# Output projection by Strassen's seven products, as a stage of its own behind the input projection, with low weight parts kept in DRAM

## The chip, the cores and the metric

The kernel runs on one core of a Trainium2 chip. The metric is the device time of one execution in microseconds; lower is better. TensorE (PE) multiplies, VectorE (DVE), ScalarE (ACT) and GpSimd (POOL) do the elementwise work, and SyncE (SP) issues the DMAs, which move data between DRAM and on-chip SBUF.

## The reference

One decoder layer in float32 on x, 2048 rows by 2048 channels. Cut to what matters:

```python
proj = einsum("bsd,de->bse", x, w_in) + b_in          # 2048 x 2048 times 2048 x 5376
c_val, c_glu, c_gate, q, k, v, a_gate = split(proj)
y_conv = conv_branch(c_val, c_glu) * silu(c_gate)     # depthwise conv of width 31, LayerNorm, silu
y_attn = windowed_attention(q, k, v, sinks) * silu(a_gate)
y = concatenate([y_conv, y_attn])                     # 2048 x 2048
y = einsum("bse,ed->bsd", y, w_out) + b_out           # 2048 x 2048 times 2048 x 2048
return layer_norm(2 ** 0.25 * x + y, ln_g, ln_b)
```

## The kernel before

The rows are worked off in four chunks of 512 (`SC`). A chunk has 84 steps of input projection and 32 steps of output projection, and then the next chunk follows. Every step takes one weight tile of 128 x 1024 float32 and has 24 matmuls of 128 x 128 by 128 x 512.

**High and low parts.** Each float32 operand is split into a high part (`copy` on ACT, rounded to fp32r) and a low part (`lo_part`: the value minus the high part, L117). A product is three matmuls (`mm3`, L527 to L529): high by high, high by low, low by high. Weights come in whole (`load_w`, 3 buffers `wr`), and `split_w` makes `wh` on ACT (L114) and `wl` on POOL for the input projection and on DVE for the rest, 3 buffers each. Every weight of the input projection is so loaded and split once a chunk, four times in all.

**Input projection.** Eight `first` steps make four column tiles side by side in four PSUM banks; 76 `in` steps then make one column tile in two steps each. `evac_in` takes a finished tile out of PSUM. Attention blocks are put between steps by the table `att`; convolution and norm work stands in a background queue `bg`, from which `run_bg` takes a few pieces a step.

**Output projection.** The products y (`ys`, high and low parts, 16 tiles each) stay in SBUF. For each of four column blocks of 512, eight steps accumulate 4 row tiles of 128 over all 16 tiles of y (`out_mm`). `evac_out` adds PSUM to the prepared 2^0.25 x + b_out (L409) and takes its statistics (L412). After a chunk, `out_norm` puts 16 norm units (ACT, DVE L436, POOL L437, store L441) into `bg`, so they run in the next chunk's first steps. In the very last column block the row tiles are finished one after the other, each with its own `tail_norm`.

**Buffers and queues.** 69 slots of 128 x 512 float32 hold everything that isn't a weight. All DMAs are issued by SP, in one order; each engine's instructions are issued in one order too. The main loop runs at each step n:

```python
list(load_w(n + 3))
split_w(n + 2)
```

## Time and profile before

| | |
|---|---|
| median of 3 runs | 2747.06 us (2746.41 to 2747.39) |
| the profiled execution: its time / its span | 2745.35 us / 2743.6 us |
| PE busy | 2696.2 us, 98% of the span |
| DVE, ACT, POOL busy | 71%, 41%, 41% |
| DMA | 308.53 MB, 112 GB/s over the span |
| weight tiles loaded, 512 KB each | 464: 336 for `w_in` (84 a chunk), 128 for `w_out` |

Busy shares are averages over the span. An engine that is idle costs nothing unless another waits for it; so the table says which engine is loaded, and the waits say what the time hangs on.

### The profile page before, as it was taken

The page shows a single profiled execution, that of the slowest core. Times are in us where ns is not written, and L with a number is a line of the kernel's source. Part 1 is how long each engine was busy: PE and PEld are TensorE (multiplying, and loading weights), DVE is VectorE, ACT ScalarE, POOL GpSimd, SP SyncE. Part 2 cuts the span into 40 slices and gives each one's busy share as a digit, 9 for nine tenths or more (in the row PEclk, how much of TensorE's full clock was granted, in tenths as well). Part 3 has the DMA queues.
Part 4 walks back from the last instruction along what each step waited for, and adds up shares of the span by engine and source line. Part 5 has one row for each costly group of instructions (what it writes and reads, how often), then busy time and mean ns, then how long its engine had stood idle before and what let it go on. Part 6 is the DMA issues. An engine that isn't in the chain of part 4 may idle for free.

```text
span 2743.6 us, 33348 instructions
## 1 busy us (share of the span) xinstructions
PE 2696.2 (98%) x12448; PEld 2243.1 (82%) x12448; DVE 1952.4 (71%) x2986; ACT 1120.5 (41%) x2060; POOL 1118.7 (41%) x632
## 2 busy tenths in 40 slices
PE   9999999999999999999999999999999999999996
PEld 7888888888788888878878888887887888888885
DVE  5587877754857887775585779777457677986827
ACT  4344454522434445442243443544233345444422
POOL 2455555200645555610064555560006455556002
PEclk9999999999999999999999999999999999999998
DMA  5222222364422222235442222224544222222424
GB/s 179 96 89 85 79 91 92 100 208 145 148 91 92 85 78 93 85 129 189 142 153 87 90 77 85 92 86 147 171 150 146 85 92 85 77 92 86 158 99 142
DMA packets 101826, 308.53 MB, mean 112 GB/s; under 512 B 11296, under 2 KB 11424, under 8 KB 101664
## 3 DMA queue, kind: packets, MB, share of 16 engines
q1 hardware_dynamic: 101664, 306.40, 33.2%
q8 instruction: 98, 1.61, 0.2%
q14 instruction: 64, 0.52, 0.1%
HBM read 289.58 MB, written 16.78 MB: 112 GB/s over the span
## 4 chain that ended last, share of the span: by engine, by line
PE 90%; DVE 4%; issue 2%; ACT 2%; POOL 1%; DMA 1%; SPq 0%; DVEq 0%; POOLq 0%
PE in L529 21%; PE in L527 21%; PE in L528 21%; PE out L527 7%; PE out L529 7%; PE out L528 7%; PE pv L334 2%; PE sc L284 1%; PE sc L285 1%; PE pt L311 1%; POOL vsum L248 1%; DMA xn<-in_x_dram 1%; DVE wl L117 1%; DVE xn L436 0%; DVE xn L565 0%
## 5 line engine op out<-in xcount | busy, mean ns | idle before, releaser
L529 PE MATMUL in<-xh,wl 128*128 128x512 f32 x2688 | 1050.3, 391 | 10.9 <-DVE wl L117 10.9
L527 PE MATMUL in<-xh,wh 128*128 128x512 f32 x2688 | 1053.8, 392 | 5.6 <-ACT xh L114 5.6
L528 PE MATMUL in<-xl,wh 128*128 128x512 f32 x2688 | 1049.5, 390 | 0.0
L117 POOL TENSOR_TENSOR wl<-wr,wh 128x1024 fp32r<-128x1024 f32 x304 | 746.7, 2459 | 637.6 <-ACT wh L114 602.9
L114 ACT ACTIVATE wh<-wr 128x1024 fp32r<-128x1024 f32 (+1 forms) x467 | 488.6, 1050 | 824.8 <-PE out L529 345.8
L203 DVE SCALAR_TENSOR_TENSOR cv<-h,cst,cv 128x512 f32<-128x512 f32 x896 | 632.1, 746 | 2.3
L529 PEld LDWEIGHTS in<-xh,wl 128*128 128x128 f32 x2688 | 505.8, 188 | 119.1 <-DVE wl L117 12.6
L527 PEld LDWEIGHTS in<-xh,wh 128*128 128x128 f32 x2688 | 506.5, 188 | 106.2 <-ACT xh L114 5.6
L528 PEld LDWEIGHTS in<-xl,wh 128*128 128x128 f32 x2688 | 506.1, 188 | 101.6 <-DVE xl L117 0.5
L117 DVE TENSOR_TENSOR wl<-wr,wh 128x1024 fp32r<-128x1024 f32 (+1 forms) x163 | 214.1, 1316 | 255.3 <-ACT wh L114 250.7
L437 POOL TENSOR_TENSOR xn<-xn,b 128x512 f32<-128x512 f32 x48 | 85.8, 1819 | 582.9 <-DVE xn L436 582.9
L527 PE MATMUL out<-wh,yah 128*128 128x512 f32 x512 | 199.7, 391 | 4.0 <-DVE xn L409 4.0
L528 PE MATMUL out<-wl,yah 128*128 128x512 f32 x512 | 199.3, 389 | 0.0
L527 PE MATMUL out<-wh,ych 128*128 128x512 f32 x512 | 199.2, 389 | 0.0
L528 PE MATMUL out<-wl,ych 128*128 128x512 f32 x512 | 199.2, 389 | 0.0
L529 PE MATMUL out<-wh,ycl 128*128 128x512 f32 x512 | 199.2, 389 | 0.0
L529 PE MATMUL out<-wh,yal 128*128 128x512 f32 x512 | 198.6, 389 | 0.0
L299 ACT ACTIVATE pr<-pr,sm 128x128 f32<-128x128 f32 x256 | 99.8, 391 | 165.9 <-DVE sm L295 165.9
L527 PEld LDWEIGHTS out<-wh,yah 128*128 128x128 f32 x512 | 96.1, 188 | 27.1 <-DVE xn L409 6.3
L529 PEld LDWEIGHTS out<-wh,yal 128*128 128x128 f32 x512 | 96.1, 188 | 20.1
L529 PEld LDWEIGHTS out<-wh,ycl 128*128 128x128 f32 x512 | 96.1, 188 | 20.0
L527 PEld LDWEIGHTS out<-wh,ych 128*128 128x128 f32 x512 | 96.1, 188 | 20.0
...
## 6 DMA issues: line engine op xcount, KB each, us to landing
wr<-in_w_in_dram SPq DMA_DIRECT2D x304, 512.0 KB, 3.2
wr<-in_w_out_dram SPq DMA_DIRECT2D x128, 512.0 KB, 3.3
...
wr<-in_w_first_dram SPq DMA_DIRECT2D x31, 512.0 KB, 3.7
...
```

The lines of the kernel that those rows point to most:

```text
L114: A.activation(out=dst, in_=src, func=AF.Copy)
L117: eng.tensor_tensor(out=dst, in0=src, in1=hi.bitcast(F32), op=ALU.subtract)
L203: V.scalar_tensor_tensor(out=o, in0=h[:, t:t + SC], scalar=wt(t), in1=a, op0=ALU.mult, op1=ALU.add)
L248: G.tensor_tensor(out=s, in0=st["vsum"], in1=q, op=ALU.add)
L284: T.matmul(o, qs[:, b * P:(b + 1) * P], ks[kv][:, b * P:b * P + 256], start=True, stop=False)
L285: T.matmul(o, qs[:, b * P:(b + 1) * P], kl[kv][:, b * P:b * P + 256], start=False, stop=True)
L299: A.activation(out=p3[:, u, :], in_=p3[:, u, :], func=AF.Exp, scale=HD ** -0.5, bias=sm[:, 1, u:u + 1], accum_out=sm[:, 3, u:u + 1])
L334: T.matmul(o, l, m, start=(n == 0), stop=(n == len(mm) - 1))
L437: G.tensor_tensor(out=z, in0=z, in1=st["b", d], op=ALU.add)
L527: T.matmul(o, lh, mh, start=start, stop=False)
L528: T.matmul(o, lh, ml, start=False, stop=False)
L529: T.matmul(o, ll, mh, start=False, stop=stop)
```

## The change

The step order becomes four chunks of 84 input steps, and behind them 112 output steps. The output stage has two blocks of 1024 rows. In a block, y and `w_out` are cut into halves by rows, by the inner dimension and by columns; seven products of half size (in the order 1, 2, 6, 7, 4, 5, 3) take the place of eight. Each product has 8 steps (two column blocks `dp` of 512, four steps `p` each), of 24 matmuls.

- y goes to DRAM (`store_y`), and `gen_y` loads what a product needs, adds or subtracts it, and splits the sum, for the product after the one that runs.
- The sums of weight quarters are made in the chunks 1 to 3 (`tsum_part`, POOL and ACT) and kept in DRAM with the low parts of all seven operands (`tsum`, `olo`).
- The low parts of the input weights are made in chunk 0 only and stored (`wlo`); later chunks load them (`load_lo`), as does the output stage.
- `evac_out` adds a product to the one or two results that take it; 8 finished tiles of a block wait in DRAM (`zd`) for their norm. Two groups of four banks take turns.
- The last four column tiles of a chunk are made side by side in 8 `last` steps, each step's weight in four DMAs, so that tiles of x come free one by one.
- Stores are issued two steps after their data is made (`store_later`).

The norms of the chunks 1, 0 and 3 begin with the third product of block 0, the first of block 1 and the third product (last in order) of block 1; that of chunk 2 is the tail.

The diff, cut to its core:

```diff
@@ -30,6 +30,8 @@
 KT = D // P
 NSLOT = 69
+PRODS = (1, 2, 6, 7, 4, 5, 3)
...
-    def four_banks(name):
+    def left_banks(name):
         return [f(f"{name}_{i}") for i, f in enumerate((acc_bank, acc_bank, cv_bank, cv_bank))]
+    def score_banks(name):
+        sc = ps_sc.tile([P, 2, 512], F32, tag="sc", name=f"{name}_s")
+        return [sc[:, 0, :], sc[:, 1, :]]
+    def right_banks(name):
+        return score_banks(name) + [ps_pt.tile([P, 512], F32, tag="pt", name=f"{name}_t"),
+                                    ps_pv.tile([P, 512], F32, tag="pv", name=f"{name}_v")]
...
             return f
-        bg_late = []
-        bg.extend(fin(j) for j in range(8))
+        st["fins"] = [fin(j) for j in range(8)]
...
-                ys[c, e] = (slot(f"yah{c}_{e}", F32R), slot(f"yal{c}_{e}", F32R))
-            hi, lo = ys[c, e]
-            V.tensor_tensor(out=o[:, i, :], in0=o[:, i, :], in1=st["ag", e][:, cols], op=ALU.mult)
-            copy(hi[:, cols], o[:, i, :])
-            lo_part(V, lo[:, cols], o[:, i, :], hi[:, cols])
+                yr[c, e] = slot(f"ya{c}_{e}")
+            V.tensor_tensor(out=yr[c, e][:, cols], in0=o[:, i, :], in1=st["ag", e][:, cols], op=ALU.mult)
+            if b == NB - 1:
+                store_y(c, e, yr.pop((c, e)))
...
-    def evac_out(c, d, s, ps):
-        z = st["z", c, s, d] = st["xn", s]
-        V.tensor_tensor(out=z, in0=z, in1=ps, op=ALU.add)
...
+    def load_xn(c, s, d):
+        t = st["zx", c, s, d] = slot(f"xn{c}_{s}_{d}")
+        r = c * SC + s * P
+        nc.sync.dma_start(out=t, in_=x[r:r + P, d * 512:(d + 1) * 512])
...
+    def z_done(c, s, d, spill=False):
+        z = st["z", c, s, d] = st.pop(("zx", c, s, d))
+        if ("bn", c, s) not in st:
+            st["bn", c, s] = small.tile([P, 4, 6], F32, tag="bn", name=f"bn{c}_{s}", bufs=16)
         V.bn_stats(out=st["bn", c, s][:, d, :], in_=z)
+        if spill:
+            t = zd[c, s, d] = dram.tile([P, 512], F32, tag=f"zd{c}_{s}_{d}", name=f"zd{c}_{s}_{d}")
+            store_later(t, st.pop(("z", c, s, d)))
...
+    def evac_out(blk, i, dp, tp):
+        ps = st["banks", dp][tp]
+        c11, c12, c21, c22 = (2 * blk, tp, dp), (2 * blk, tp, dp + 2), (2 * blk + 1, tp, dp), (2 * blk + 1, tp, dp + 2)
+        if i == 1:
+            u = st["U", dp, tp] = slot(f"U{blk}_{dp}_{tp}")
+            copy(u, ps)
+            add(st["zx", *c11], ps)
+        elif i == 2:
+            add(st["zx", *c11], ps)
+            z_done(*c11, spill=True)
+        elif i == 6:
+            add(st["U", dp, tp], ps)
+            add(st["zx", *c12], st["U", dp, tp])
+        elif i == 7:
+            u = st.pop(("U", dp, tp))
+            add(u, ps)
+            add(st["zx", *c21], u)
+            add(st["zx", *c22], u)
+        elif i == 4:
+            add(st["zx", *c21], ps)
+            z_done(*c21)
+        elif i == 5:
+            add(st["zx", *c12], ps)
+            add(st["zx", *c22], ps)
+            z_done(*c22)
+        else:
+            add(st["zx", *c12], ps)
+            z_done(*c12)
...
+    NEW = {1: ((0, 0),), 6: ((0, 2),), 7: ((1, 0), (1, 2))}
+    yd = {(c, e): dram.tile([P, 512], F32, tag=f"y{c}_{e}", name=f"yd{c}_{e}") for c in range(NCH) for e in range(16)}
...
+    def store_later(dst, src):
+        later.append((st["n"] + 2, lambda: nc.sync.dma_start(out=dst, in_=src)))
...
+    TAKES = {1: ((0, 0),), 2: ((0, 8),), 6: ((1, 0), (1, 8), (0, 0)), 7: ((0, 0), (1, 0)), 4: ((1, 8),),
+             5: ((1, 0), (1, 8)), 3: ((0, 8), (0, 0))}
+    def load_y(blk, i, k):
+        r = yraw[blk, i, k] = []
+        for h, e in TAKES[i]:
+            t = slot(f"yr{blk}_{i}_{k}_{len(r)}")
+            nc.sync.dma_start(out=t, in_=yd[2 * blk + h, e + k])
+            r.append(t)
...
+    def gen_y(blk, i, k):
+        t, *more = yraw.pop((blk, i, k))
+        ops = {6: (ALU.add, ALU.subtract), 7: (ALU.subtract,), 5: (ALU.add,), 3: (ALU.add, ALU.subtract)}.get(i, ())
+        if i == 3:
+            more.append(st.pop(("S", k)))
+        for op, b in zip(ops, more):
+            V.tensor_tensor(out=t, in0=t, in1=b, op=op)
+        if i == 5:
+            st["S", k] = t
+        hi, lo = yc[blk, i, k] = slot(f"yh{blk}_{i}_{k}", F32R), slot(f"yl{blk}_{i}_{k}", F32R)
+        copy(hi, t)
+        lo_part(V, lo, t, hi)
...
+    def tsum_load(dp, p, kk):
+        w = slice(kk * 512, kk * 512 + 512)
+        b = st["tb", dp, p, kk] = [slot(f"tb{dp}_{p}_{kk}_{n}") for n in range(4)]
+        for t, (d, q) in zip(b, ((dp, p), (dp + 2, p), (dp, 4 + p), (dp + 2, 4 + p))):
+            nc.sync.dma_start(out=t, in_=w_out[d, q][:, w])
...
+    def tsum_part(dp, p, kk, i):
...
+        t = {1: b11, 2: b21, 3: b22, 5: b11, 7: b12, 6: b22, 4: b21}[i]
+        ab = {5: (b12, b11), 7: (b22, b12), 6: (b22, b11), 4: (b21, b22)}.get(i)
+        if ab:
+            G.tensor_tensor(out=t, in0=ab[0], in1=ab[1], op=ALU.subtract)
+            store_later(tsum[i, dp, p][:, w], t)
+        hi, lo = slot(f"th{dp}_{p}_{kk}_{i}", F32R), slot(f"tl{dp}_{p}_{kk}_{i}", F32R)
+        copy(hi, t)
+        lo_part(G, lo, t, hi)
+        store_later(olo[i, dp, p][:, w], lo.bitcast(F32))
...
             load_gb(c, 0)
+            for d, s in units[:2]:
+                load_z(c, s, d)
         def fin(n):
             def f():
+                if n + 2 < 16:
+                    d, s = units[n + 2]
+                    load_z(c, s, d)
...
-        for t in range(4, len(ORDER)):
-            steps += [("in", c, t, *ORDER[t], hf) for hf in range(2)]
-        for d in range(4):
-            for p in range(8):
-                steps.append(("out", c, d, p))
-    raws, splits = {}, {}
-    def w_src(s):
+        steps += [("in", c, t, *ORDER[t], hf) for t in range(4, 38) for hf in range(2)]
+        steps += [("last", c, p) for p in range(8)]
+    OUT0 = len(steps)
+    prods = [(blk, i) for blk in range(2) for i in PRODS]
+    steps += [("out", blk, i, dp, p) for blk, i in prods for dp in range(2) for p in range(4)]
+    TAIL = len(steps) - 4
...
+        if s[0] == "last":
+            p = s[2]
+            return [(slice(t * 256, t * 256 + 256), w_in[34 + t, p // 4][:, p % 4 * 256:p % 4 * 256 + 256])
+                    for t in range(4)]
+        _, _, i, dp, p = s
+        if i in (1, 2, 3):
+            return [(whole, w_out[dp + (2 if i == 3 else 0), p + (0 if i == 1 else 4)])]
+        return [(whole, tsum[i, dp, p])]
...
+    def lo_src(n):
+        s = steps[n]
+        return olo[s[2:]] if s[0] == "out" else wlo[n % PER]
+    def load_lo(n):
+        if PER <= n <= TAIL and n not in los:
+            t = los[n] = wspl.tile([P, 1024], F32R, tag="wl", name=f"wl{n}")
+            nc.sync.dma_start(out=t.bitcast(F32), in_=lo_src(n))
...
+        t = raws[n]
+        hi = wspl.tile([P, 1024], F32R, tag="wh", name=f"wh{n}")
+        lo = los[n] if n >= PER else wspl.tile([P, 1024], F32R, tag="wl", name=f"wl{n}")
...
+            copy(hi[:, w], t[:, w])
+            if n < PER:
+                lo_part(G if steps[n][0] != "first" else V, lo[:, w], t[:, w], hi[:, w])
+        los[n] = lo
+        splits[n] = ((hi[:, 0:512], hi[:, 512:1024]), (lo[:, 0:512], lo[:, 512:1024]))
+    def tail_w(n):
...
+            w = slice(i * 512, i * 512 + 512)
+            nc.sync.dma_start(out=raw[i], in_=src[:, w])
+            nc.sync.dma_start(out=lo[i].bitcast(F32), in_=low[:, w])
+        splits[n] = (hi, lo)
+        st["tailw", n] = lambda: [copy(h, r) for h, r in zip(hi, raw)]
...
+        for p in range(8):
+            for k in (2 * p, 2 * p + 1):
+                if c + 1 < NCH:
+                    at(base + 77 + p, load_x, c + 1, k)
+                    at(base + 78 + p, split_x, c + 1, k)
+                elif p < 4:
+                    at(base + 78 + p, load_y, 0, PRODS[0], k)
+                    at(base + 79 + p, gen_y, 0, PRODS[0], k)
+    for j in range(16):
+        job = (j // 8, j // 2 % 4, j % 2)
+        n = PER + 10 + 14 * j
+        at(n, tsum_load, *job)
+        for k, i in enumerate((1, 2, 3, 5, 7, 6, 4)):
+            at(n + 3 + k, tsum_part, *job, i)
+    for m, (blk, i) in enumerate(prods[1:]):
+        for k in range(8):
+            at(OUT0 + 8 * m + k - (k > 0), load_y, blk, i, k)
+            at(OUT0 + 8 * m + k, gen_y, blk, i, k)
...
         else:
             list(load_w(n + 3))
+            load_lo(n + 2)
             split_w(n + 2)
+        if n < PER:
+            store_later(wlo[n], los[n].bitcast(F32))
...
-                st["acc"] = four_banks(f"in{c}")
-            for kk in range(2):
-                k = 2 * p + kk
-                xh, xl = xs[c, k]
+            if p == 0 and s[0] == "first":
+                st["acc"] = [acc_bank(f"in{c}_{i}") for i in range(2)] + score_banks(f"in{c}")
+            elif p == 0:
+                st["acc"] = right_banks(f"in{c}l")
...
+            elif p == 7:
                 for t in range(4):
-                    cols = slice(t * P, (t + 1) * P)
-                    mm3(st["acc"][t], hi[kk][:, cols], lo[kk][:, cols], xh, xl, k == 0, k == KT - 1)
-            if p == 7:
-                for t in (1, 0, 2, 3):
-                    evac_in(c, t, *ORDER[t], st["acc"][t])
+                    evac_in(c, 38 + t, *ORDER[38 + t], st["acc"][t])
+                run_all()
+                bg.extend(st["fins"])
...
-            _, c, d, p = s
-            if d == 0 and p == 0:
-                run_bg(len(bg))
...
+                st["banks", dp] = (left_banks if dp else right_banks)(f"out{blk}_{i}_{dp}")
+            for h, d in NEW.get(i, ()):
+                if p == 0:
+                    st["bo", d] = bcast_row(b_out, dp + d, f"bo{blk}_{i}_{dp}_{d}")
+                else:
+                    scale_xn(2 * blk + h, p - 1, dp + d, st["bo", d])
+                load_xn(2 * blk + h, p, dp + d)
+            tail = n >= TAIL
             if not tail:
-                for i in range(4):
-                    out_mm(c, n, p, i)
...
+            for f, *args in late:
+                f(*args)
+            late = []
+            if p == 3 and not tail:
+                late = [(scale_xn, 2 * blk + h, 3, dp + d, st["bo", d]) for h, d in NEW.get(i, ())]
+                late += [(evac_out, blk, i, dp, tp) for tp in range(4)]
+            if dp == 0 and p == 0:
+                if i == 3:
+                    bg.extend(out_norm(2 * blk + 1))
+                elif i == 1 and blk == 1:
+                    bg.extend(out_norm(0))
+            run_bg(3)
+            if TAIL - 6 <= n < TAIL - 3:
+                tail_w(n + 7)
+            if TAIL - 3 <= n < TAIL:
+                st["tailw", n + 4]()
+                if n == TAIL - 1:
+                    for d in range(4):
+                        load_gb(c, d)
+            if TAIL - 8 <= n < TAIL:
+                load_z(2, (n - TAIL + 8) // 2, (n - TAIL + 8) % 2)
+            if n == len(steps) - 1:
+                run_all()
+                for tp in range(4):
+                    for m in range(TAIL, TAIL + 4):
+                        out_mm(m, (tp,))
+                    evac_out(blk, i, dp, tp)
+                    tail_norm(2, tp)
```

## Rows read from the trace of the kernel before

**Rows 1.** The page's first part: span, and PE's busy time.
```profile
span 2743.6 us, 33348 instructions
PE 2696.2 (98%) x12448; PEld 2243.1 (82%) x12448; DVE 1952.4 (71%) x2986; ACT 1120.5 (41%) x2060; POOL 1118.7 (41%) x632
```
**Rows 2.** The page's chain that ended last, shares by engine.
```profile
PE 90%; DVE 4%; issue 2%; ACT 2%; POOL 1%; DMA 1%; SPq 0%; DVEq 0%; POOLq 0%
```
**Rows 3.** Timeline of PE, first and last of 57 matmuls: start, duration.
```profile
599.61 0.39 PE L527 MATMUL out<-wh,yah 128*128 128x512 f32 x1
...
612.30 0.39 PE L529 MATMUL out<-wh,yal 128*128 128x512 f32 x1
```
**Rows 4.** Waits of PE: total us, times, longest.
```profile
PE in L529 <- DVE wl L117: 10.9, 4, 3.5
...
PE out L527 <- DVE xn L409: 4.0, 5, 0.9
```
**Rows 5.** Timeline of PE at one long gap; 7 matmuls lie between the last two.
```profile
710.68 0.39 PE L528 MATMUL in<-xl,wh 128*128 128x512 f32 x1
714.53 0.73 PE L529 MATMUL in<-xh,wl 128*128 128x512 f32 x1 [3.47 <-DVE wl L117]
...
718.05 0.40 PE L528 MATMUL in<-xl,wh 128*128 128x512 f32 x1
```
**Rows 6.** The page's DMA queue: packets, MB, share of 16 engines.
```profile
q1 hardware_dynamic: 101664, 306.40, 33.2%
```
**Rows 7.** Stretches: busy us by engine, PE's granted clock, DMA share, GB/s.
```profile
10.00:12.00 2.00, 2.00 (x7) 1.63 (x6) 1.65 (x5) 2.00 (x6) 0.00 (x0) 1.00 1.04 408
10.00:20.00 10.00, 10.00 (x42) 8.21 (x41) 6.63 (x11) 6.57 (x13) 0.00 (x0) 1.00 0.94 333
560.00:570.00 10.00, 10.00 (x46) 8.29 (x45) 8.02 (x11) 3.75 (x5) 0.00 (x0) 1.00 0.91 309
200.00:210.00 10.00, 10.00 (x47) 8.31 (x46) 3.96 (x7) 3.61 (x13) 5.29 (x3) 1.00 0.24 75
710.00:720.00 10.00, 6.53 (x22) 4.91 (x21) 10.00 (x7) 1.06 (x1) 9.37 (x7) 0.83 0.56 184
720.00:1230.00 510.00, 508.56 (x2394) 424.81 (x2393) 385.18 (x610) 228.25 (x453) 254.15 (x139) 1.00 0.28 94
```
**Rows 8.** DMA issues: count, size, median us to landing.
```profile
wr<-in_w_in_dram SPq DMA_DIRECT2D x304, 512.0 KB, 3.2
```
**Rows 9.** Timeline of SP: three DMAs issued back to back.
```profile
561.56 1.38 SPq L172 DMA_DIRECT2D xr<-in_xT_dram  x3
```
**Rows 10.** Waits of SP's queue: total us, times, longest.
```profile
SPq L487 <- POOL wl L117: 1600.2, 286, 10.4
...
SPq L441 <- POOL xn L437: 56.5, 45, 2.0
```
**Rows 11.** Groups by line and shape: busy us, mean ns of one.
```profile
L117 POOL TENSOR_TENSOR wl<-wr,wh 128x1024 fp32r<-128x1024 f32 x304 | 746.7, 2459 | 637.6 <-ACT wh L114 602.9 <-PE pv L334 21.5 <-PE sc L285 12.2
...
L436 DVE TENSOR_TENSOR xn<-xn,g 128x512 f32<-128x512 f32 x48 | 69.1, 1502 | 0.0
...
L117 DVE TENSOR_TENSOR xl<-xr,xh 128x512 fp32r<-128x512 f32 x64 | 43.0, 688 | 20.2 <-PE out L528 11.6 <-ACT xh L114 8.3
L409 DVE TENSOR_TENSOR xn<-xn,out 128x512 f32<-128x512 f32 x64 | 42.2, 679 | 5.9 <-PE out L529 4.5
L412 DVE BATCH_NORM_STATS2 bn<-xn 128x6 f32<-128x512 f32 x64 | 41.6, 683 | 0.1
...
L140 ACT ACTIVATE cgate_5t<-in,half 128x512 f32<-128x512 f32 x4 | 2.7, 680 | 0.0
```
**Rows 12.** Timeline of the tail: two of DVE's four evictions, PE's last matmul.
```profile
2702.18 0.69 DVE L409 TENSOR_TENSOR xn<-xn,out 128x512 f32<-128x512 f32 x1 [4.48 <-PE out L529]
...
2711.65 0.68 DVE L409 TENSOR_TENSOR xn<-xn,out 128x512 f32<-128x512 f32 x1
...
2722.16 0.39 PE L529 MATMUL out<-wh,ycl 128*128 128x512 f32 x1
```

More of the change, by code (lines that the diff above doesn't have):

```diff
@@ L148, in hybrid_layer_kernel @@
     xs = {}
-    ys = {}
+    yr = {}
+    yraw = {}
+    yc = {}
     bg = deque()
+    later = []
     st = {}
@@ new lines, in hybrid_layer_kernel @@
+    pieces = [(dp, p) for dp in range(2) for p in range(4)]
+    tsum = {(i, *q): dram.tile([P, 1024], F32, tag=f"T{i}_{q}", name=f"T{i}_{q[0]}_{q[1]}")
+            for i in (5, 6, 7, 4) for q in pieces}
+    olo = {(i, *q): dram.tile([P, 1024], F32, tag=f"O{i}_{q}", name=f"O{i}_{q[0]}_{q[1]}")
+           for i in range(1, 8) for q in pieces}
+    wlo = [dram.tile([P, 1024], F32, tag=f"wlo{n}", name=f"wlo{n}") for n in range(84)]
+    def tsum_load(dp, p, kk):
[3 more added lines that the diff above has]
+            nc.sync.dma_start(out=t, in_=w_out[d, q][:, w])
@@ L481, in load_w @@
     def load_w(n, parts=1):
-        if n >= len(steps) or n in raws:
+        if n >= len(steps) or n in raws or n > TAIL:
             return
         t = raws[n] = wraw.tile([P, 1024], F32, tag="raw", name=f"wr{n}")
+        for cols, src in w_src(n):
+            for i in range(parts):
+                w = slice(i * 1024 // parts, (i + 1) * 1024 // parts) if parts > 1 else cols
+                nc.sync.dma_start(out=t[:, w], in_=src[:, w] if parts > 1 else src)
+                yield
+    def lo_src(n):
+        s = steps[n]
+        return olo[s[2:]] if s[0] == "out" else wlo[n % PER]
@@ L486, in load_w @@
             w = slice(i * 1024 // parts, (i + 1) * 1024 // parts)
-            nc.sync.dma_start(out=t[:, w], in_=w_src(steps[n])[:, w])
-            yield
-    def split_w(n, parts=1, in_slots=False):
-        if n >= len(steps) or n in splits:
-            return
-        t = raws[n]
-        eng = G if steps[n][0] == "in" else V
-        if in_slots:
-            hi, lo = ([slot(f"w{x}{n}_{i}", F32R) for i in range(2)] for x in "hl")
-            parts = 2
-        else:
-            hi, lo = (wspl.tile([P, 1024], F32R, tag=f"w{x}", name=f"w{x}{n}") for x in "hl")
-        for i in range(parts):
-            w = slice(i * 1024 // parts, (i + 1) * 1024 // parts)
-            h, l = (hi[i], lo[i]) if in_slots else (hi[:, w], lo[:, w])
-            copy(h, t[:, w])
-            lo_part(eng, l, t[:, w], h)
-        splits[n] = (hi, lo) if in_slots else ((hi[:, 0:512], hi[:, 512:1024]), (lo[:, 0:512], lo[:, 512:1024]))
+            copy(hi[:, w], t[:, w])
@@ new lines, in split_w @@
+            if n < PER:
[3 more added lines that the diff above has]
+    def tail_w(n):
+        raw, hi, lo = ([slot(f"w{x}{n}_{i}", F32 if x == "r" else F32R) for i in range(2)] for x in "rhl")
+        src, low = w_src(n)[0][1], lo_src(n)
+        for i in range(2):
+            w = slice(i * 512, i * 512 + 512)
[3 more added lines that the diff above has]
+        st["tailw", n] = lambda: [copy(h, r) for h, r in zip(hi, raw)]
@@ L509, in hybrid_layer_kernel, with at @@
     att = {}
-    per = 84 + 32
+    def at(n, *what):
+        att.setdefault(n, []).append(what)
     for c in range(NCH):
-        base = c * per
+        base = c * PER
         for r in range(4):
@@ L583, in hybrid_layer_kernel @@
     split_x(0, 1)
+    late = []
     for n, s in enumerate(steps):
+        st["n"] = n
         c = s[1]
-        tail = c == NCH - 1 and s[0] == "out" and s[2] == 3
+        for when, f in later:
+            if when <= n:
+                f()
+        later[:] = [x for x in later if x[0] > n]
         if c == 0 and s[0] == "first":
@@ L644, in hybrid_layer_kernel @@
         else:
[L645 to L647 removed]
+            _, blk, i, dp, p = s
             if p == 0:
[L649 to L655 removed]
@@ L686, in hybrid_layer_kernel @@
+        if n < TAIL:
             raws.pop(n, None)
             splits.pop(n, None)
+            los.pop(n, None)
+            if s[0] == "last":
+                for kk in range(2):
+                    xs.pop((c, 2 * s[2] + kk))
+            elif s[0] == "out" and dp:
+                for kk in range(2):
+                    yc.pop((blk, i, 2 * p + kk))
     run_bg(len(bg))
+    for _, f in later:
+        f()
 _ARRAYS = ["x", "xT", "w_first", "w_in", "w_out", "consts", "b_out", "ln_g", "ln_b"]
```

120 lines of the change are left out of this document (55 added, 65 removed).

## The prediction, written before the result was known

> **What bounds the kernel now.** The page's first part comes first: PE is busy for 98% of the span [rows 1]. A busy PE need not be a full one, so the chain that ended last is read next; 90% of it is PE's own work [rows 2]. The timeline of PE then gives the price of one matmul: 57 in a row start within 12.69 us, so 56 steps of 0.2266 us [rows 3]. The before kernel has 4 x 84 x 24 = 8064 of them in the input projection and 4 x 32 x 24 = 3072 in the output projection, together 2523 us; attention and a few others fill the rest. So the number of matmuls sets the time, and what else there is to gain are gaps.
>
> The waits of PE name few: 10.9 us in four waits for a low weight part made on DVE, and 4.0 us in five waits for a bank that DVE had to empty [rows 4]. The timeline at such a gap shows the whole price: from 710.68 to 718.05 there are nine starts, 7.37 us where 2.04 would do, because the matmuls behind the gap start 0.43 us apart at first; the granted clock of that stretch is 0.83, that is, part of it at 1.2 and not 2.4 GHz [rows 5, 7]. So one gap costs 5.3 us. Three of the four waits are of this kind (the norm of a finished chunk keeps DVE busy just when DVE should split the first weights of the next), together 16 us; the fourth is short.
>
> DMA is far from its limit: 33.2% of the 16 engines [rows 6].
>
> **The change part by part.**
>
> *Matmuls.* The output stage has 2 x 7 x 8 x 24 = 2688 in place of 3072; 384 x 0.2266 = **-87.0 us**. The input stage keeps its 8064 and all of attention.
>
> *Gaps removed.* From the second chunk on no low part of a weight is made on DVE any more; it is loaded. The three gaps go: **-16 us**. Bank turns in the output stage now leave an emptied bank 4 steps (21.7 us) of time, so the 4.0 us go too: **-4 us**.
>
> *New turn of banks at the output stage's start.* The four banks of the `last` tiles are the first banks of product 1. ACT empties them with 8 reads of 0.68 us, 5.4 us [rows 11]; PE would want the fourth bank 3 x 3 x 0.2266 = 2.0 us after the first: **+3.4 us**. Bounds are 0 (ACT starts before the last bank is done) and 5.4. At the three other turns PE first has 12 matmuls (2.7 us) on two other banks, while ACT's four reads of the banks it wants next take 2.7: nothing.
>
> *Work on other engines.* 228 of POOL's 304 low parts and 152 of DVE's 160 go; POOL gets 16 x 11 pieces of half the size for the sums. POOL was 41% busy and mostly waits [rows 1, 11], so this gains and costs nothing; without that cover, a late sum would still have some 100 us until its product. In the output stage DVE has per block 88 additions, 32 statistics, 48 sums and 56 low parts of y, 32 scalings and 16 to 32 norm products: about 270 to 290 pieces of 0.68 to 1.5 us [rows 11], some 220 us in 304 us of matmuls. Hidden.
>
> *DMA in the input stage.* A step of 5.44 us loads 0.52 MB more (or stores it, in chunk 0): 96 GB/s on top of 94 [rows 7], with sums, y and x some 250. PE lost no matmul in a stretch with 309 GB/s: 46 starts in 10 us, the same pace as elsewhere [rows 7]. Hidden, nothing.
>
> *DMA in the output stage.* This is the term that decides. A product's 8 steps take 8 x 24 x 0.2266 = 43.5 us and load 8 x 1.05 = 8.4 MB of weights, high and low. To this come tiles of 0.262 MB: 8 to 24 of y for the next product, 8 to 16 of x with 2 to 4 of b_out (products 1, 6, 7), 8 spilled (product 2), and 24 for a norm (16 stores, 8 of gamma and beta), 32 where spilled tiles come back. The last two products also hold the tail's weights and what its norm needs. In the order of the products this is 13.1, 15.7, 16.3, 15.7, 12.6, 12.6, 16.8 MB in block 0 and 21.5, 15.7, 16.3, 15.7, 12.6, 15.7, 13.1 MB in block 1: 213 MB in 609 us, 350 GB/s, and 494 in block 1's first product. The rate that the engines reach has these rows: 408 in the best 2 us; 333 at a share of 0.94, so 354, over the first dense 10 us; 309 at 0.91, so 340; 306.40 MB in 33.2% of 2743.6 us, so 336, on the mean; 75 at 0.24, so 312, in a quiet stretch [rows 6, 7]. I take 354, the longest dense stretch. A low part is issued when the matmuls of two steps before its own end (its buffer is then free), 10.9 us ahead, and lands in 3.2 us when it is quiet [rows 8]: PE stands only for what a queue is late beyond 7.6 us. At 354 the products are late by (MB / 0.354 - 43.5), carried on: 4.2 us up to product 7 of block 0, worked off in 4 and 5, 3.9 after its last, then 60.7 - 43.5 = 17.2 more, so 21.1 and a stand of 13.5; with the 7.6 still open, the next three products add 0.9, 2.4, 0.9. Together **+17.7 us**. The same sum gives 1.6 at 408, 34.7 at 336, 70.4 at 312.
>
> By the Trainium skill, page "DMA: Bandwidth & Descriptors", section "Specifications", a core's share of HBM is about 358 GB/s. By that the same sum would be 15 us, and no stretch of this trace is long enough to show a plateau there.
>
> *Issue.* Three DMAs take SP 1.38 us [rows 9], 0.46 each. Even the first step of block 1 has no more than 12 to 14, under 6.5 us; a mean step has 5.4. Nothing at the mean.
>
> *Tail.* DVE's chain for a row tile takes 9.47 us [rows 12] and so outlasts PE's share, which falls from 30 matmuls (6.80 us) to 24 (5.44). From the first tile's end on the tail lasts as before, 41.4 us, while three tiles of PE time lie beside it: 4.1 us less hidden. On top, the norm of chunk 3 has 19 pieces at three a step and only four steps before the tail, so 5 to 7 units of 1.5 us may stand ahead of the first eviction on DVE [rows 11]: up to 7.5 more. I take **+6**, between 4.1 and 11.6, nearer the lower, because DVE has idle time there.
>
> *Sum.* -87.0 - 16 - 4 + 3.4 + 17.7 + 6 = -79.9. The profiled execution took 2745.35 us for a span of 2743.6, so 2665; the median of the runs shown lies 1.7 above it: **2667 us**.
>
> **The rivals.**
>
> *Norms block the queue.* SP issues in one order, and behind each norm store that waits for POOL stand the next weights, low parts and y. In the before trace SP waits 56.5 us for POOL's norm results in 45 waits, 18.8 us a norm [rows 10]. There the loads behind had time. If both norms in the middle of the output stage let the DMA engines stand for 18.8 us, products 3 of block 0 and 1 of block 1 take that much longer, and the carried sum is 55.4 in place of 17.7: 2705 us. For it: these are the two fullest products. Against: the engines still have up to several transfers under way while SP waits. The page "DMA: Bandwidth & Descriptors" of the Trainium skill, section "Anatomy of one DMA", says that DMA engines never wait on semaphores and that any wait happens on the issuing sequencer; [rows 10] agree.
>
> *DMA keeps up.* If a long stretch holds the 408 GB/s of the best 2 us, 1.6 us remain of 17.7: 2651 us. For it: more transfers are in flight than ever before. Against: the 10 us behind that stretch.
>
> The same page of the Trainium skill, section "Bandwidth", has 425 GB/s for one 16 MB transfer; by that nothing of the term would be left.
>
> *Slower than before: the output stage is paced by DMA throughout.* Without its DMA term the change gains 97.6 us. The carried sum eats this up at 299 GB/s. So it decides if SP's lockstep with PE (each step's low part waits for a buffer, and all behind it waits too) leaves the engines idle for more than 16% of the stage at 354. At 22%, 276 GB/s, the stage alone is 773 us for 609 and the carried sum 157: some 2806 us. For it: SP waits 1600 us for low parts before [rows 10]. Against: those waits were free because a load stayed 3.2 us under way with 10 to spare.
>
> **How the numbers follow.** Forecast, stands of 8 to 27 us in the output stage: 0.45. Blocked queue or 312 to 340 GB/s, 2680 to 2728 us: 0.24. DMA keeps up, 2646 to 2658: 0.19. Paced by DMA and not faster: 0.12, of which 0.02 within 0.2%, about what a measurement of this kernel can tell from no change. The low end is -87.0 - 20 + 0 + 1.6 + 4.1 = -101.3 against the median, 2646. The high end is -87.0 - 20 + 5.4 + 70.4 + 11.6 = -19.6, 2727; this leaves out the last case and a bit of the second. Most cases are on one side, so one range stands. Faster 0.88, same 0.02, slower 0.10.
>
> **What would show it.** PE has 12064 matmuls in place of 12448, at 0.2266 us in both stages, and no long gap in the first steps of the chunks 1 to 3. Output products without a norm take 43 to 45 us; the first of block 1 takes 55 to 60, with a DMA share near 1 and PE waiting for a low part's or a weight's DMA. At the output stage's start PE waits some 3 us for ACT. The prediction is wrong if products without a norm take over 46 us, if the input stage gets longer than 4 x 508 us (a late store or low part), if PE's pace per matmul changes, or if the tail behind PE's last matmul, 21 us before [rows 1, 12], passes 30.

## The result, and the profile after

The changed kernel takes 2715.67 us (median of 4 runs, 2714.82 to 2716.59), before 2746.73 (4 runs, 2745.88 to 2747.39): the ratio is 0.9887, with a 95% interval of 0.9870 to 0.9904. It is faster by 31 us (1.1%); 80 were forecast. The direction and the range held, the size is less than half. The profiled execution took 2715.71 us, its span is 2714.0 us.

The page after: span and busy times, the chain by engine, the DMA queue, the bytes. They answer to [rows 1, 2, 6].

```profile
span 2714.0 us, 34597 instructions
PE 2615.7 (96%) x12064; PEld 2176.0 (80%) x12064; DVE 1836.1 (68%) x2992; ACT 1191.4 (44%) x2125; POOL 786.8 (29%) x580
...
q1 hardware_dynamic: 254592, 671.37, 72.5%
...
HBM read 543.33 MB, written 127.93 MB: 247 GB/s over the span
...
PE 70%; DVE 5%; DMA 3%; ACT 1%; issue 1%; SPq 0%; POOL 0%; DVEq 0%; ACTq 0%
```

The 384 matmuls are gone and PE is busy for 80.5 us less, but the chain runs through PE for 70% of the span and no longer for 90%. Twice the bytes are moved. The waits of PE after (total us, times, longest) say what came in, beside [rows 4]:

```profile
PE out_s L718 <- ACT wh L125: 15.3, 2, 13.7
PE out L719 <- DMA wl<-O: 13.1, 4, 10.1
PE in L720 <- DMA wl<-wlo: 9.7, 3, 4.4
PE in L718 <- ACT xh L125: 5.5, 1, 5.5
PE in_s L718 <- ACT cgate_5t L151: 2.2, 1, 2.2
```

The waits for low parts made on DVE and for banks that DVE empties are gone, as forecast. New ones stand in their place. Taking the starts of the matmuls from PE's timeline, the span splits like this (us):

| | before | after | change | forecast |
|---|---|---|---|---|
| up to the first matmul | 5.6 | 5.5 | -0.1 | 0 |
| input projection, four chunks | 2014.4 | 2017.7 | +3.3 | -16 |
| output: its matmuls at 0.2266 | 696.1 | 609.1 | -87.0 | -87.0 |
| output: all else | 6.3 | 36.7 | +30.4 | -4 + 3.4 + 17.7 = +17.1 |
| behind the last matmul | 21.3 | 45.0 | +23.7 | +6 |

Of the 14 output products, 10 take 43.5 us, bare matmul pace. The first takes 45.2. Product 3 of block 0 takes 59.2, product 1 of block 1 takes 61.1 and product 2 behind it 45.2. What a product takes beyond 43.5 is called its stand: PE stands and waits. So the stands are in the two places where a norm runs, which the forecast named as the fullest; but their causes are two, as the experiments show.

*Product 3 of block 0.* SP's timeline (start, duration in which the group was issued) and, below it, the waits of SP and ACT from 2311 to 2345 us. Stores `out_dram<-xn` that wait for POOL stand ahead of the weights `wr` and `wl`:

```profile
2298.19 0.33 SPq L638 DMA_DIRECT2D wr<-in_w_out_dram  x1
...
2307.70 0.33 SPq L649 DMA_DIRECT2D wl<-O  x1
...
2317.41 5.43 SPq L570 DMA_DIRECT2D out_dram<-xn  x4
...
2328.15 5.02 SPq L570 DMA_DIRECT2D out_dram<-xn  x3
2333.26 0.38 SPq L638 DMA_DIRECT2D wr<-in_w_out_dram  x1
2333.74 0.40 SPq L649 DMA_DIRECT2D wl<-O  x1
```
```profile
SPq L570 <- POOL xn L566: 19.2, 14, 3.1
...
ACT wh L125 <- DMA wr<-in_w_out_dram: 5.7, 1, 5.7
```

Between two `wr` lie 35 us, where a step of PE needs one each 5.44 us. PE's timeline shows the end of it, and the windows show that the DMA engines meanwhile were not full (share 0.82 and 0.88):

```profile
2338.80 0.80 PE L718 MATMUL out_s<-wh,yh 128*128 128x512 f32 x1 [13.68 <-ACT wh L125]
```
```profile
2286.00:2329.00 43.00, 39.12 (x173) 32.07 (x171) 36.94 (x61) 22.05 (x30) 17.56 (x11) 1.00 0.82 257
2329.00:2345.00 16.00, 6.20 (x20) 5.03 (x21) 12.17 (x13) 2.37 (x4) 8.65 (x6) 0.58 0.88 281
```

PE's wait names ACT's copy of a weight, but ACT only waited for the load that SP had not issued. The name in a wait is the last link of a chain, not its cause.

*Product 1 of block 1.* Here the DMA engines are full: share 0.94 to 1.02 while PE is fed and while it stands (2370 to 2380). The fourth row is the whole product, the last a stretch of product 2 behind it.

```profile
2350.00:2360.00 10.00, 10.00 (x46) 8.29 (x45) 4.19 (x21) 7.59 (x11) 0.00 (x0) 1.00 1.02 309
2360.00:2370.00 10.00, 8.88 (x40) 7.01 (x38) 6.52 (x7) 5.76 (x9) 4.89 (x3) 1.00 0.94 321
2370.00:2380.00 10.00, 1.00 (x2) 0.83 (x3) 9.98 (x8) 3.29 (x5) 8.74 (x7) 0.65 1.00 313
2345.00:2406.00 61.00, 46.62 (x193) 37.11 (x192) 41.91 (x60) 27.16 (x36) 25.93 (x16) 0.92 1.00 342
2410.00:2420.00 10.00, 10.00 (x46) 8.29 (x45) 3.16 (x5) 2.61 (x3) 0.00 (x0) 1.00 1.03 398
```

*Behind the last matmul.* DVE's timeline: eleven pieces of chunk 3's norm (L565, multiplication by gamma) stand ahead of the first eviction (L440) of the tail's four row tiles, five more and the tail's own pieces (L758) ahead of the last two, whose last matmul started at 2668.81 [rows 12]:

```profile
2649.10 11.50 DVE L565 TENSOR_TENSOR xn<-xn,g 128x512 f32<-128x512 f32 x8
...
2662.43 3.42 DVE L565 TENSOR_TENSOR xn<-xn,g 128x512 f32<-128x512 f32 x3
2665.78 0.67 DVE L440 TENSOR_TENSOR xn<-xn,out 128x512 f32<-128x512 f32 x1
...
2675.14 0.68 DVE L565 TENSOR_TENSOR xn<-xn,g 128x512 f32<-128x512 f32 x1
2675.74 1.75 DVE L758 SCALAR_TENSOR_TENSOR zl<-zl,tw,b 128x512 f32<-128x512 f32 x1
2677.41 6.75 DVE L565 TENSOR_TENSOR xn<-xn,g 128x512 f32<-128x512 f32 x4
...
2688.55 0.67 DVE L440 TENSOR_TENSOR xn<-xn,out 128x512 f32<-128x512 f32 x1
...
2689.21 0.67 DVE L440 TENSOR_TENSOR xn<-xn,out 128x512 f32<-128x512 f32 x1
```

### The profile page after: what moved, and what is told of

It is laid out like the page before. It is cut to its first block, busy times and chain, and to the rows that moved or that the text cites. A ratio compares the mean times of both kernels' runs of the same rounds, so it can differ in the third digit from the quotient of the medians.

```text
span 2714.0 us, 34597 instructions
## 1 busy us (share of the span) xinstructions
PE 2615.7 (96%) x12064; PEld 2176.0 (80%) x12064; DVE 1836.1 (68%) x2992; ACT 1191.4 (44%) x2125; POOL 786.8 (29%) x580
## 4 chain that ended last, share of the span: by engine, by line
PE 70%; DVE 5%; DMA 3%; ACT 1%; issue 1%; SPq 0%; POOL 0%; DVEq 0%; ACTq 0%
PE in L720 14%; PE in L719 14%; PE in L718 14%; PE out L719 3%; PE out L720 3%; PE out L718 3%; PE pv L343 2%; PE out_s L719 2%; PE out_s L720 2%; PE out_s L718 2%; DVE xn L565 2%; PE sc L293 1%; PE sc L294 1%; PE out_t L719 1%; PE out_v L720 1%; PE out_v L719 1%
## 5 line engine op out<-in xcount | busy, mean ns | idle before, releaser
L718 PE MATMUL in<-xh,wh 128*128 128x512 f32 x2304 | 904.5, 393 | 7.6 <-ACT xh L125 5.5
L720 PE MATMUL in<-xh,wl 128*128 128x512 f32 x2304 | 901.4, 391 | 9.7 <-DMA wl<-wlo 9.7
L719 PE MATMUL in<-xl,wh 128*128 128x512 f32 x2304 | 900.6, 391 | 0.0
L128 POOL TENSOR_TENSOR wl<-wr,wh 128x1024 fp32r<-128x1024 f32 x76 | 185.4, 2441 | 194.8 <-ACT wh L125 176.2
L128 POOL TENSOR_TENSOR tl<-tb,th 128x512 fp32r<-128x512 f32 x112 | 156.9, 1414 | 253.4 <-ACT th L125 236.5
L719 PE MATMUL out<-wl,yh 128*128 128x512 f32 x448 | 176.8, 395 | 13.1 <-DMA wl<-O 13.1
L720 PE MATMUL out<-wh,yl 128*128 128x512 f32 x448 | 175.8, 393 | 0.0
L718 PE MATMUL out<-wh,yh 128*128 128x512 f32 x448 | 165.8, 390 | 0.0
L128 POOL TENSOR_TENSOR plc<-pmc,phc 128x512 fp32r<-128x512 f32 x64 | 85.1, 1330 | 171.4 <-ACT phc L125 170.3
L719 PEld LDWEIGHTS out<-wl,yh 128*128 128x128 f32 x448 | 85.3, 190 | 32.6 <-DMA wl<-O 14.8
```

The lines of the kernel that those rows point to most:

```text
L128: eng.tensor_tensor(out=dst, in0=src, in1=hi.bitcast(F32), op=ALU.subtract)
L718: T.matmul(o, lh, mh, start=start, stop=False)
L719: T.matmul(o, lh, ml, start=False, stop=False)
L720: T.matmul(o, ll, mh, start=False, stop=stop)
```

## The experiments

All start from the changed kernel. The table gathers what each run took (us; the products by block and number, the others take 43.5 to 47.3, but for e4; "behind" is the time behind the last matmul).

| run | time | input | 0/3 | 1/1 | 1/2 | 1/6 | behind |
|---|---|---|---|---|---|---|---|
| after | 2715.67 | 2017.7 | 59.2 | 61.1 | 45.2 | 43.5 | 45.0 |
| e1_ready_stores | 2696.99 | 2015.6 | 43.5 | 59.5 | 45.3 | 43.5 | 44.7 |
| e2_pool_queue | 2704.37 | 2019.7 | 43.5 | 63.5 | 43.7 | 43.5 | 46.9 |
| e3_no_norm_3 | 2701.35 | 2019.5 | 60.4 | 60.5 | 45.8 | 43.5 | 24.1 |
| e4_extra_loads | 2739.91 | 2016.7 | 66.2 | 61.4 | 44.9 | 43.5 | 44.9 |
| e5_add_on_dve | 2700.31 | 2016.0 | 52.8 | 59.1 | 44.1 | 43.5 | 41.0 |
| e6_spread | 2697.09 | 2018.1 | 43.7 | 43.5 | 43.5 | 59.4 | 45.4 |
| e7_y_later | 2709.91 | 2011.9 | 60.0 | 60.2 | 45.3 | 44.3 | 44.6 |
| e8_all_three | 2681.7 | 2008.4 | 43.5 | 43.5 | 43.5 | 60.5 | 39.0 |
| e9_fewer_bytes | 2706.43 | 2016.3 | 60.3 | 51.3 | 43.5 | 43.5 | 46.2 |
| e10_all_and_fewer | 2673.58 | 2013.2 | 43.5 | 43.5 | 43.5 | 45.9 | 38.8 |
| e11_early_gb | 2669.8 | 2013.1 | 43.5 | 43.5 | 43.5 | 45.8 | 35.6 |
| e12_row_copies | 2713.28 | 2018.7 | 59.7 | 59.0 | 45.2 | 43.5 | 44.2 |
| e13_all | 2667.3 | 2013.3 | 43.5 | 43.5 | 43.5 | 46.3 | 34.2 |

Only after, e11 and e13 have several runs behind their time; in the others a difference of 2 us in all says nothing (the four runs of after spread over 1.8). Parts scatter more: the runs whose edits leave the input projection alone have it between 2015.6 and 2019.7.

**Stores that never wait.**

```diff
+        if ready:
+            z = vt.rearrange("p a b c -> p (a b c)")[:, 0:512].bitcast(F32)
...
-                    store(c, s, d)
+                    store(c, s, d, ready=c < 3)
```

> The norm stores of the chunks 1 and 0 take their bytes from a tile that has long been ready (vt), so those 1024 rows of the output are not the result; norms are computed all the same, and every DMA keeps its size and place. Queue theory (norm stores that wait for POOL hold SP's single order, and with it the next weights): the products of 59 and 61 us fall to 43.5 to 46, 2716 - 33 = about 2683 us. Bandwidth theory (these products ask for more bytes than the engines give, the forecast's own): both stay near 60, 2716 us. Load theory (the norm's work on DVE and POOL delays y): both stay near 60 too.

Product 3 of block 0 falls from 59.2 to 43.5 us, all of its stand; product 1 of block 1 only to 59.5. So the waiting stores are the cause in the one place and not in the other.

**The same stores through POOL's queue.**

```diff
-                    store(c, s, d)
...
+                    G.dma_start(out=out[r:r + P, d * 512:(d + 1) * 512], in_=st.pop(("z", c, s, d)))
```

> The norm stores of the chunks 1, 0 and 3 are issued from POOL, which makes their data, not from SP. Queue theory: nothing waits ahead of the weights in SP's order; the two slow products fall to 43.5 to 46 and the time to about 2683 us, some us less if the tail's loads come earlier too. Bandwidth theory: no change, 2716 us. Against both: if issuing costs POOL about 1 us each, the norm takes POOL 16 us longer, and the tail can grow by up to that.

The same split: 43.5 and 63.5. The order on SP, not the stores as such, made product 3 stand.

**No norm of chunk 3.**

```diff
-                if i == 3:
-                    bg.extend(out_norm(2 * blk + 1))
+                if i == 3 and blk == 0:
+                    bg.extend(out_norm(1))
```

> The norm of chunk 3 is left out, so its 512 rows are not written; all else stays. If that norm is what lengthens the tail (its units stand ahead of the last evictions on DVE and POOL, its gamma and beta loads ahead of the tail's), the time behind PE's last matmul falls from 45.0 us to the 21.3 of before plus 4 for the shorter PE share, 25: about 2696 us. If the tail is long for another reason (late weights, evictions in turn with two bank groups), it stays above 40: 2714 us.

Behind the last matmul 24.1 us remain of 45.0. The norm of chunk 3 costs 20.9 there, the other edits of the tail 2.8 over before's 21.3.

**More loads.**

```diff
+            if blk == 0 and i in (2, 6, 7, 4, 5):
+                for q in range(2):
+                    nc.sync.dma_start(out=slot(f"ex{n}_{q}"), in_=w_out[q, p][:, 0:512])
```

> In block 0, every step of the products 2, 6, 7, 4 and 5 loads two more tiles of 0.262 MB that nothing reads. This puts 2, 6, 7 at 458 to 471 GB/s and 4, 5 at 386. If the engines hold some 405 GB/s: 2, 6, 7 are late by 5.6, 7.0, 5.6 us, of which 7.6 fits into the slack, so PE stands 8 to 13 us in 6 and 7 (and the third product may move by a few), 4 and 5 take 43.5. With 354 GB/s: also 4 and 5 late, 45 to 60 us more in all. If SP's issue or the eight transfers under way set the limit and not bytes, 4 and 5 stretch as well.

Products 2, 6 and 7 of block 0 take 43.5, 54.9 and 49.7 us. Windows (the products 2 to 7, this run; then the same products of the changed kernel, which lose nothing):

```profile
2065.00:2213.00 148.00, 136.28 (x577) 109.28 (x576) 75.32 (x118) 41.51 (x51) 0.00 (x0) 0.98 1.03 389
```
```profile
2063.00:2194.00 131.00, 130.97 (x578) 108.46 (x579) 75.15 (x119) 42.45 (x53) 0.00 (x0) 1.00 1.00 368
```

The engines carry 389 GB/s over 148 us where a stretch of 10 us with 354 was the longest dense one before [rows 7]. So 354 was not a limit for these loads. Nor were 405 reached over that stretch: products 6 and 7 stand for 11.4 + 6.2 = 17.6 us, more than the 8 to 13 of that theory. The 358 GB/s that the Trainium skill gives as a core's share of HBM ("DMA: Bandwidth & Descriptors", "Specifications") is passed too, by the one core that runs here.

**The add of beta on DVE in place of POOL.**

```diff
-        G.tensor_tensor(out=z, in0=z, in1=st["b", d], op=ALU.add)
+        V.tensor_tensor(out=z, in0=z, in1=st["b", d], op=ALU.add)
```

> The last step of a norm's unit, z + b (16 units a norm), goes from POOL to DVE; loads, stores and their order in the program stay. Theory A: what stands in products 3 of block 0 and 1 of block 1 is DVE slowed by POOL's add (in the changed kernel DVE's multiplication by g took 1.44 to 1.77 us beside POOL's add, 0.67 alone): the norm's pass then costs DVE 1.35 us a unit and no other DVE instruction is slowed, so both products (59.2 and 61.1 us) come down to 44 to 48 us, and the time behind the last matmul from 45 to about 35 us; time about 2680 us. Theory B: the burst of gamma, beta and z loads ahead of the weights is what stands in product 1 of block 1: that product stays at 57 to 62 us, only product 3 of block 0 falls (its stores wait for the adds); about 2695 us. Rival: DVE, with 16 more instructions of 0.67 us in a product, becomes late itself: no gain, 2710 us or more.

Product 1 of block 1 stays (59.1): theory A falls there. Product 3 loses 6.4 us and the tail 4.0, although DVE has 16 more pieces a norm. The groups of DVE by shape show why, first in the changed kernel (2312 to 2345 us), then in this run (2280 to 2345); busy us, mean ns:

```profile
L565 DVE TENSOR_TENSOR xn<-xn,g 128x512 f32<-128x512 f32 x14 | 19.6, 1454 | 0.0
L128 DVE TENSOR_TENSOR yl<-yr,yh 128x512 fp32r<-128x512 f32 x6 | 7.5, 1257 | 1.7 <-ACT yh L125 1.7
```
```profile
L566 DVE TENSOR_TENSOR xn<-xn,b 128x512 f32<-128x512 f32 x16 | 10.4, 680 | 0.0
L565 DVE TENSOR_TENSOR xn<-xn,g 128x512 f32<-128x512 f32 x16 | 10.3, 680 | 0.0
L128 DVE TENSOR_TENSOR yl<-yr,yh 128x512 fp32r<-128x512 f32 x12 | 8.2, 686 | 8.3 <-ACT yh L125 8.3
```

Beside POOL's adds a multiplication takes 1454 ns; without them it takes 680 and the add 680. Two pieces on DVE alone cost less than one on DVE beside one on POOL. (The Trainium skill, "SBUF — State Buffer", "SBUF: two separate sides", says that an instruction of DVE with two SBUF inputs and one of GpSimd that reads SBUF shut each other out. The 1454 fit that; a mean alone does not tell shutting out from sharing.)

**The norms of chunks 1 and 0 spread thinner.**

```diff
-            run_bg(3)
+            run_bg(3 if blk == 1 and i == 3 else 1)
```

> In the output stage one piece of a norm is queued per step of 8 products' weights instead of three (three again in the very last product): the norms of chunks 1 and 0 take 19 steps each instead of 7. Theory A and theory B both say that products 3 of block 0 and 1 of block 1 come down to 44 to 48 us (from 59.2 and 61.1), with about 2686 us in all and the tail unchanged at 45 us. Rival: the work is only moved, and products 2 and 6 of block 1, which now share it, stand: their sum over 87 us grows by as much as the two others fall, 2705 us or more.

Both stands vanish, and one of 15.9 us comes up in product 6 of block 1: of 35.0 us (15.7 + 17.6 + 1.7) some 19 are gained. That is near the 15.7 of the stores; what full DMA engines cost seems only to be moved. PE waits there for low parts at a share of 1.03:

```profile
2400.00:2420.00 20.00, 16.53 (x73) 13.34 (x72) 10.90 (x15) 6.17 (x9) 3.26 (x2) 1.00 1.03 362
2420.00:2440.00 20.00, 17.96 (x67) 14.60 (x68) 13.54 (x19) 8.61 (x12) 6.19 (x4) 0.83 1.03 388
2440.00:2460.00 20.00, 14.82 (x60) 11.80 (x59) 16.18 (x22) 5.27 (x7) 10.68 (x5) 0.91 1.03 381
```

**Stores of y later.**

```diff
-        store_later(yd[c, e], t)
+        later.append((st["n"] + 4, lambda: nc.sync.dma_start(out=yd[c, e], in_=t)))
```

> The stores of y are queued four steps after they are named instead of two. Theory: at the starts of chunks 2 and 3 TensorE stands 4.6 us each, with 1.6 us of lower clock behind each, because the loads of low parts stand behind stores of y that wait for DVE: both gaps go, input chunks 502.7, 504.3 and 504.7 us become about 502, 498 and 499; about 2704 us. Rival: the gaps come from loads of the next chunk's x and of weights that are late anyway: no change, 2713 to 2717 us.

The input projection falls by 5.8 us, about half of the some 12 that were expected. It is no scatter: the five runs with this edit have 2008.4 to 2013.3, all others 2015.6 or more. PE's waits from 510 to 2010 us, after and then here:

```profile
PE in L720 <- DMA wl<-wlo: 9.7, 3, 4.4
...
PE vT L398 <- ACT vraw L394: 0.7, 2, 0.4
```
```profile
PE vT L398 <- ACT vraw L394: 5.8, 2, 3.4
...
PE in L720 <- DMA wl<-wlo: 0.9, 1, 0.9
```

The late low parts are gone; 5.1 us of the 8.8 come back as a wait for ACT, next in line. What the low parts stood behind in the changed kernel are the waits of SP's stores (1040 to 1055 us):

```profile
SPq L481 <- DVE cn_6u L281: 2.5, 1, 2.5
SPq L481 <- DVE cn_5u L281: 2.5, 1, 2.5
```

The gap was a queue's; behind it stood an engine's.

**All three.** The edits of e5, e6 and e7, and the tail takes the gamma and beta of chunk 3's norm.

```diff
-                if n == TAIL - 1:
-                    for d in range(4):
-                        load_gb(c, d)
```

> The three edits together, and the last norm (chunk 2) takes the gamma and beta that chunk 3's norm has loaded, 8 loads fewer in the last product. If the causes are separate: 14 us each from products 3 of block 0 and 1 of block 1, 10 us from the chunk starts, 10 to 15 us from behind the last matmul: 2660 to 2668 us. If one cause stands behind several: about 2680 us. Rival: holding tiles longer delays the loads that need their place: over 2690 us.

2681.7 us: 19 from the output products, 9.3 from the input, 6.0 from the tail, 34 together, and not the 48 to 56 of causes that add up. Product 6 of block 1 keeps its stand. Of the 9.3 a part is likely scatter: e10, e11 and e13, with the same stores of y, have 2013.1 to 2013.3, a gain of 4.5.

**Fewer bytes.**

```diff
-            z_done(*c11, spill=True)
+            z_done(*c11, spill=blk == 1)
...
     def load_gb(c, d):
+        if c == 0:
+            return
```

> From the changed kernel with one thing done: block 0 keeps its z instead of storing 8 tiles and loading them back, and chunk 0's norm takes the gamma and beta that chunk 1's has loaded; product 1 of block 1 so moves 17.3 MB instead of 21.5 (16 loads of 0.26 MB fewer) and product 2 of block 0 2.1 MB fewer. Theory of the bytes: product 1 of block 1 falls from 61.1 to 44 to 49 us, product 3 of block 0 stays at 59; about 2702 us. Theory of the norm's own work (the pass on ACT, DVE and POOL makes weights late): product 1 of block 1 stays at 57 us or more; about 2713 us.

Products 1 and 2 of block 1 lose 9.8 + 1.7 = 11.5 us with 4.2 MB; at 0.389 MB per us that is 10.8. Product 3 of block 0 stays. Bytes are most of the price there; what the 7.8 us that remain are, the norm's own work or another thing, stays open.

**All and fewer.** The edits of e8 and e9 together.

> The version with all three edits and the tail's gamma and beta, with block 0's z kept and chunk 0's gamma and beta taken from chunk 1 as well: products 1, 2 and 6 of block 1 then move about 49.3 MB instead of 53.5. Theory of the bytes: the stand of 16 us in product 6 of block 1 falls to 5 us or less; about 2668 us. Rival: stores to memory are what is slow there, and they stay: 10 us or more stand; about 2678 us.

Product 6 of block 1 falls from 60.5 to 45.9, a stand of 2.4, as the theory of the bytes has it; the time misses its 2668 because the input projection takes 4.8 us longer than in e8. The windows of its products 1, 2 and 6 give 17.0 + 15.2 + 18.3 = 50.5 MB in 133 us; in e6 the same three took 146 us:

```profile
2325.00:2368.00 43.00, 43.00 (x192) 35.61 (x191) 40.59 (x82) 27.23 (x39) 0.00 (x0) 1.00 1.03 395
2368.00:2412.00 44.00, 44.00 (x196) 36.46 (x195) 29.61 (x48) 12.20 (x16) 0.00 (x0) 1.00 0.96 345
2412.00:2458.00 46.00, 44.27 (x194) 36.02 (x193) 28.13 (x46) 15.32 (x19) 0.00 (x0) 1.00 1.04 398
```

In the last of these windows 11 stores are issued, 7 of them a norm's, and the rate is 398 GB/s. So stores among the loads are not slow as such, and the rival falls. In e6 the 59 us of the same product had 13 stores, 9 of them a norm's, and went at 383:

```profile
2416.00:2475.00 59.00, 48.03 (x192) 38.40 (x191) 47.56 (x58) 18.62 (x24) 29.85 (x16) 0.91 1.03 383
```

**Gamma and beta earlier.**

On top of e10:

```diff
+            if n in (TAIL - 8, TAIL - 7):
+                load_gb(3, n - TAIL + 8)
```

> The same, and the first two gamma and beta pairs of the last norm are loaded one product earlier. If DVE's first multiplication of chunk 3's norm waits for them (10 us between its statistics and it), the time behind the last matmul falls from 39 to about 30 us; about 2660 us in all. Rival: DVE's order, not the loads, holds it: the time behind the last matmul stays at 37 to 40 us, no gain over the run before.

2669.8 us (5 runs, 2668.84 to 2670.08), ratio to before 0.9717 (0.9704 to 0.9730). Behind the last matmul 35.6, not 30. DVE starts the norm's units 14.5 us into the last product (23.6 in e8), and is then full: busy for 27.3 of the 28 us from 2604 to 2632. The 16 units are done only just before the first two row tiles are evicted, 2.1 us ahead of PE's last matmul (2632.47), though the first tile's matmuls end three tiles, 16.3 us, earlier:

```profile
2603.72 0.69 DVE L568 TENSOR_TENSOR xn<-xn,g 128x512 f32<-128x512 f32 x1 [0.89 <-ACT xn L567]
...
2630.40 1.28 DVE L440 TENSOR_TENSOR xn<-xn,out 128x512 f32<-128x512 f32 x2
```

**Rows copied out once.** `spread_row` loads each row of gamma, beta and bias to 128 partitions once, in the chunks 1 to 3, and stores it; `bcast_row` loads that copy.

```diff
+    for j in range(12):
+        at(PER + 22 + 14 * j, spread_row, (ln_g, ln_b, b_out)[j % 3], j // 3, f"sr{j}")
```

> From the changed kernel with one thing done: each row of gamma, beta and the output bias (12 rows of 2 KB) is spread over the 128 partitions once, in chunk 1, stored to memory as 128 rows, and loaded from there later (28 loads in the output stage are of the same bytes as before, but read 128 different rows). Theory: the loads that read one row 128 times hold the engines full at a low rate (2350 to 2370 us: share 0.94 to 1.02 at 309 to 321 GB/s, where loads without them reach 404 GB/s at 1.04), so product 1 of block 1 with 8 such loads of 0.26 MB falls from 61.1 to 50 to 56 us, the time behind the last matmul from 45 to about 42; about 2703 us, and no window at a share over 1.0 is under 370 GB/s. Rival: the low rate is that of loads and stores mixed, whatever rows they read: no change beyond 3 us.

The rate in the window of the loads rises from 309 to 395 GB/s, but the product only falls by 2.1 us, no more than single runs differ:

```profile
2350.00:2360.00 10.00, 10.00 (x46) 8.29 (x45) 4.07 (x19) 7.80 (x11) 0.00 (x0) 1.00 1.04 395
2360.00:2370.00 10.00, 8.40 (x38) 6.61 (x36) 8.61 (x7) 6.26 (x9) 6.70 (x4) 1.00 0.89 306
2370.00:2380.00 10.00, 4.47 (x11) 3.51 (x12) 10.00 (x9) 3.32 (x4) 9.15 (x6) 0.67 1.01 334
```

In this window the loads of one row 128 times are the slow ones; the low rate later, when the norm's stores come in a burst, has another cause, which was not found. The theory names a true effect and misses the size.

**All with the row copies.** The edits of e11 and e12 together.

> The same on top of the version with every edit so far (2669.8 us). Theory: products 7 and 2 to 6 lose their last 4 us of standing, the tail up to 2 us: 2663 to 2667 us. Rival: nothing there waits for these loads now: 2668 to 2671 us; the 12 stores and loads in chunk 1 could even cost: over 2671 us.

2667.3 us (4 runs, 2664.21 to 2672.62), ratio 0.9708 (0.9692 to 0.9725): no different from e11. Both beat both kernels.

## Why the prediction was right in direction and wrong in size

- *Matmuls, -87.0.* Right: 12064 matmuls, and 10 products at 43.5 us.
- *DMA in the output stage, +17.7.* The term held where it was put: products 1 and 2 of block 1 stood for 17.6 + 1.7 = 19.3 us with full engines, and e9 shows that mostly bytes did it. That it came out near is in part luck. The rate was not one: 389 to 404 in stretches with plain loads, 342 over the 61 us of product 1 of block 1, where a whole norm's loads and stores come in a burst (spread thinner, they went at 383 and 398 in e6 and e10), and 354 lies between. And with e9's 17.3 MB the same sum would leave 1.7 us (an estimate: 3.9 + 48.9 - 43.5 - 7.6), where 7.8 stood. The carried sum at 354 gave 13.5, 0.9, 2.4 and 0.9 us for products 1, 2, 6 and 7 of block 1, where 17.6, 1.7, 0 and 0 were measured.
- *Missed: the stores on SP.* Product 3 of block 0 was to be late by 3.9 us, within the slack of 7.6. It stood for 15.7. The step that failed is "at 354 the products are late by (MB / 0.354 - 43.5)", which takes the queue to be always open. The rival "norms block the queue" has this mechanism, and e1 and e2 show it; its place was half right: it holds for the norm of chunk 1, not for that of chunk 0. The time lies in the case that had 0.24, which holds this rival and a lower rate. The argument against it, that several transfers are still under way, is no help: 35 us passed between two loads of weights, and PE's whole lead was 7.6.
- *Gaps removed, -16.* DVE's low parts no longer hold PE, but the projection got 3.3 us longer. The step failed in taking a removed wait for a gap removed. At the starts of chunks 2 and 3 DVE still ends its work on `cn` late; now the stores of `cn` wait for it on SP, and the loads of low parts behind them (e7). Then ACT's `vraw` is next. At chunk 1's start PE waits 2.2 us for ACT to empty a bank of the `last` tiles, a turn that was priced only at the output stage's start. And chunk 0, which had no gap to lose, got longer (506.0 us from its first matmul to the next chunk's; before, 502.1 to the output's). e7 gives back 5.8 of the 19.3 us that this term is off; for most of the rest no experiment was made.
- *Emptied banks, -4, and the turn at the start, +3.4.* The first is right. The first product stood for 1.7 us, within the bounds of 0 to 5.4.
- *Tail, +6.* Mis-sized: +23.7. The step that failed is the count of 5 to 7 units ahead of the first eviction: the norm of chunk 3 was put at up to 7.5 us; it costs 20.9 (e3). "DVE has idle time there" failed: the norm's statistics are ready only after product 5, its gamma and beta came late, and its 16 units cost DVE about 1.4 us each beside POOL, so that 11 lie ahead of the first eviction and all 16 ahead of the last two. With the add on DVE and with earlier gamma and beta, e5, e8 and e11 come to 4.0, 6.0 and 9.4 us less than after; 14 us over before remain, with DVE full.
- *Sum of the misses:* output stage 30.4 - 17.1 = 13.3, input 3.3 + 16 = 19.3, tail 17.7, together 50.3 of the 50 us between 80 forecast and the 29.6 by which the span fell.

"What would show it" was of use: products without a norm at 43.5, product 1 of block 1 at 61.1 (55 to 60 given), and the tail over 30, named as a sign of error. 4 x 508 us for the input was too loose a test for a term of 16. What stays open is why a norm's loads and stores in a burst went at 342 GB/s, beyond the rows read 128 times, and most of what the input projection lost.
